# NSA attention of a hybrid decoder on one core: the compressed branch's values as two split products with a block-diagonal moving operand in place of four native fp32 products

## The chip, the core and the metric

The kernel runs on one core of one Trainium2 chip. Its engines work in parallel and each runs its own instructions in order: PE (TensorE, matrix products, with weight loads shown apart as PEld), DVE (VectorE), ACT (ScalarE), POOL (GpSimd), and SP, which issues transfers. Products accumulate in PSUM banks; PE, DVE and ACT can reach them. The metric is the device time of one launch in microseconds; the median of three runs was 2314.84.

## The reference

A decoder trunk of four layers on 512 tokens of width 1024: RG-LRU, native sparse attention (NSA), gated linear attention, RG-LRU, each followed by a SwiGLU channel mixer. The change touches NSA alone, layer 1. Cut to what matters there:

```python
kc = nsa_compress(k_c, ...)            # 31 compressed keys per kv group
vc = nsa_compress(v_c, ...)            # 31 compressed values per kv group, 64 wide
# for each block of 128 queries, 4 kv groups g, 4 heads h in a group:
lg_c = einsum('bqghd,bngd->bghqn', qi, kc) + head_bias(dist_c)
p_c = masked_softmax(lg_c, dist_c >= 0)
o_c = einsum('bghqn,bngd->bqghd', p_c, vc)      # the product that is changed
# o_s: selected blocks (all 8 blocks are chosen), o_w: sliding window, both over 512 keys
return gi[..., 0:1] * o_c + gi[..., 1:2] * o_s + gi[..., 2:3] * o_w
```

Each softmax weight is already multiplied by its gate before the products, so the three branches add up in one PSUM bank.

## The kernel before

Everything is computed transposed: features on partitions, 512 tokens in the free dimension. Weights stream in as blocks of 128x1024 (`wr`, `wc`), are split into a high and a low part of type fp32r by ACT and DVE (`ws`, L287 and L288), and a product of fp32 quality is three fp32r products (L329 to L331, L591 to L593). Where an operand is used unsplit, PE runs its native fp32 product.

The NSA attention loop (`attention`, `run`, L1159) goes over 32 units (g, i, br): 4 groups g of heads, 4 query blocks i, and two branches, br = 0 (selected together with compressed) and br = 1 (window). In a group the order is (3,0), (0,0), (3,1), (0,1), (2,0), (1,0), (2,1), (1,1) for (i,br). In iteration n three units are in work:

- `logits(n + 3)`: PE multiplies queries and keys (L1029, L1030; for br = 0 the 31 compressed keys lie in front of the 512 others, tile `kk`), DVE adds the bias and takes the row minimum of the negated logits (L1032, L1186), ACT takes exponentials (L1046, L1052);
- `weights(n + 2)`: DVE makes reciprocals and gate factors (L1001, L1002, L1065, L1066, L1068), POOL scales the weights L (L1060);
- `values(n)`: PE transposes the weights of 128 keys and four heads into one bank (L1116), ACT and DVE copy or split it (`ph`, `pl`: L357, L358), and up to four steps later PE multiplies the values with it into the bank `ob` (L1103, or L1105 and L1106). `store` then adds the two halves of `ob` and splits the result (L1136, L1137, L1143, L1144).

For br = 0, `values` first transposes the compressed weights of four heads (tile `lc`, four heads by 32 on the free axis) in one product (L1095), so that partition 32*hh + n holds key n of head hh, and ACT copies that to `pc` (L1097). The values of the compressed branch are `vcd`, a large tile of 128x4x4x64: for head hh, rows 32*hh to 32*hh + 31 hold the values and all other rows are zero. Four native fp32 products per unit (L1108, L1109), each with 128 moving columns, go into columns of rows 0 to 63 of `ob`.

PE's instructions of the loop stand in the order in which they are written (a manual schedule, L951). On ACT, DVE, POOL and SP a scheduler orders the instructions by its own estimate of when each is ready, and takes the tiles of a pool as they come free. The pool of large tiles has four buffers; `ktl`, `kth` (compressed keys' inputs), `vcd`, `kk` and `wc` (weight blocks that are summed during loading, of the feed-forward layers) share them. `no` and `nq` are output and query projections that fill PE inside the loop.

Of the kernel before, what the change touches and what calls it, by code (L numbers as in the profile page):

```python
# [8 lines left out]
F32 = mybir.dt.float32  # L9
F32R = mybir.dt.float32r  # L10
I32 = mybir.dt.int32
AF = mybir.ActivationFunctionType
OP = mybir.AluOpType
# [179 lines left out]
class Kernel:  # L193
# [615 lines left out]
    def nsa(self, j, nxt):  # L809
        nc, prm = self.nc, self.prm  # L810
        mm = nc.tensor.matmul
# [3 lines left out]
        nsm = self.fixed.tile([128, 256], F32, name="nsm")  # L815
# [22 lines left out]
        def hidden(kv, lo, hi):  # L838
            w1 = self.take(("raw", "w1", j, kv))
            b = self.bank("cmp")  # L840
            o = b[0:64, 0:124].rearrange("p (g n) -> p g n", n=31)
            for m in range(16):
                mm(o, lhsT=w1[:, m * 64:m * 64 + 64],
                   rhs=lo[:, m, :, 0:31] if m < 8 else hi[:, m - 8, :, 1:32], start=m == 0, stop=m == 15)
            g = gl[kv] = self.slot("gl")
            nc.gpsimd.memset(g[:, 0:128], 0.0)
            glv = g[0:64, 0:128].rearrange("p (g n) -> p g n", n=32)
            nc.scalar.activation(glv[:, :, 0:31], o, AF.Gelu_apprx_tanh, bias=prm[0:64, C_B1 + kv:C_B1 + kv + 1])
# [7 lines left out]
        def cmp_spread():  # L856
            g4 = gl[2] = self.slot("gl4")
            nc.gpsimd.tensor_copy(g4[0:64].rearrange("p (g h n) -> p g h n", g=4, h=4),
                                  gl[1][0:64, 0:128].rearrange("p (g n) -> p g n", n=32)[:, :, None, :].to_broadcast([64, 4, 4, 32]))
            nc.gpsimd.memset(vcd, 0.0)  # L860

        def cmp_values():
            b = self.bank("cmp2")
            for g in range(4):
                mm(b[:, g * 64:g * 64 + 64], lhsT=gl[2][0:64, g * 128:g * 128 + 128], rhs=nsm[0:64, 128:192], start=True, stop=True)
            for hh in range(4):
                rows = slice(hh * 32, hh * 32 + 32)
                nc.vector.tensor_tensor(vcd[rows, :, hh, :], b[rows, 0:256].rearrange("p (g d) -> p g d", d=64),
                                        nsm[rows, None, 192:256].to_broadcast([32, 4, 64]), op=OP.add)

        def gates(b):
            gf = self.slot("gf")
# [39 lines left out]
        b = self.bank("ng")  # L912
# [6 lines left out]
        at(1, cmp_keys)  # L919
        list(queries(1))  # L920
        hidden(1, *c1)
        vcd = self.large([128, 4, 4, 64], "vcd")
        cmp_spread()
        at(1, cmp_values)
        for i in range(4):
            at(i + 1, bias_rows, 4 * i)
# [14 lines left out]
        for t in range(4):  # L941
            r = self.rstd[:, t:t + 1]
            for br in range(2):
                v = V[t, br] = self.slot("v", F32R)
                vv = v.rearrange("p (g two d) -> p g two d", g=4, two=2)
# [10 lines left out]
    def attention(self, j, kc, kw, qw, V, vcd, gt, os, queries, output):  # L956
        nc, mm = self.nc, self.nc.tensor.matmul
# [37 lines left out]
        LC = [self.fixed.tile([128, 128], F32, name=f"lc{i}") for i in range(4)]  # L995
        for x in LC:
            nc.gpsimd.memset(x, 0.0)

        def weight(g, i, br, s):
            r, w = small("sr"), small("sw")  # L1000
            nc.vector.reciprocal(r, s)  # L1001
            nc.vector.tensor_tensor(w, r, gt[:, i, g * 12 + br:g * 12 + 12:3], op=OP.mult)  # L1002
            return w
# [82 lines left out]
        def values(u, es):  # L1086
            g, i, br = u
            d = st.pop(u)
# [3 lines left out]
            ob = OB[g, i]  # L1092
            if br == 0:
                b = self.bank("pc")
                nc.tensor.transpose(b[:, 0:128], d["lc"][:, 0:128], self.ident)  # L1095
                pc = self.slot("pc")
                nc.scalar.activation(pc[:, 0:128], b[:, 0:128], AF.Copy)  # L1097

            def product(jt, p):
                v = V[jt, br][:, g * 128:g * 128 + 128]  # L1100
                first, last = br == 0 and jt == 0, br == 1 and jt == i
                if len(p) == 1:
                    mm(ob, lhsT=v.bitcast(F32), rhs=p[0], start=first, stop=last)  # L1103
                else:
                    mm(ob, lhsT=v, rhs=p[0], start=first, stop=False)  # L1105
                    mm(ob, lhsT=v, rhs=p[1], start=False, stop=last)  # L1106
                if br == 0 and jt == 0:
                    for hh in range(4):  # L1108
                        mm(ob[0:64, hh * 128:hh * 128 + 128], lhsT=vcd[:, g, hh, :], rhs=pc[:, 0:128], start=False, stop=False)  # L1109

            ne = len(es)
            for jt in range(i + 1):
                b = self.bank("pt")
                for hh in range(4):
                    c = slice(hh * 128, hh * 128 + 128)
                    nc.tensor.transpose(b[:, c], L[hh][:, jt * 128:jt * 128 + 128], self.ident)  # L1116
                if NSA_AT["whole"][g] >> (jt + 4 * br) & 1:
                    p = [self.slot("p")]
# [4 lines left out]
                else:  # L1123
                    p = self.split(b, "p")
# [346 lines left out]
```

## Time and profile before

| | |
|---|---|
| median of 3 runs | 2314.84 us (2314.52 to 2316.72) |
| profiled execution, its own time | 2313.41 us |
| its span | 2311.7 us |
| PE busy | 2275.7 us (98%) |
| DVE busy | 1483.2 us (64%) |
| ACT busy | 1221.9 us (53%) |
| POOL busy | 346.9 us (15%) |
| the attention loop | about 655 to 860 us of the span |

Busy shares of the whole span mix phases with different limits: outside the attention loop PE is fed without a break, inside it three more engines are nearly full. So the loop is read by itself, from the busy time in its stretches, from the chain of waits that ended last (each piece is followed back to what released it), and from single instructions in order of time. Records of PE overlap, since products are pipelined and their ends are modelled; what one of them costs PE is the distance from its start to the next start.

### The profile page before, as it was taken

The page shows a single profiled execution, that of the slowest core. Times are in us where ns is not written, and L with a number is a line of the kernel's source. Part 1 is how long each engine was busy: PE and PEld are TensorE (multiplying, and loading weights), DVE is VectorE, ACT ScalarE, POOL GpSimd, SP SyncE. Part 2 cuts the span into 40 slices and gives each one's busy share as a digit, 9 for nine tenths or more (in the row PEclk, how much of TensorE's full clock was granted, in tenths as well). Part 3 has the DMA queues.
Part 4 walks back from the last instruction along what each step waited for, and adds up shares of the span by engine and source line. Part 5 has one row for each costly group of instructions (what it writes and reads, how often), then busy time and mean ns, then how long its engine had stood idle before and what let it go on. Part 6 is the DMA issues. An engine that isn't in the chain of part 4 may idle for free.

```text
span 2311.7 us, 29407 instructions
## 1 busy us (share of the span) xinstructions
PE 2275.7 (98%) x10898; PEld 1912.0 (83%) x10898; DVE 1483.2 (64%) x2460; ACT 1221.9 (53%) x1971; POOL 346.9 (15%) x413
## 2 busy tenths in 40 slices
PE   8999999999999999999999999999999999999998
PEld 7877888898876778888988887888898878888897
DVE  7887646466289888555466526745465886745555
ACT  5965535353468766444455435625354685635353
POOL 1001101001356531010110000101010000201010
PEclk9999999999999999999999999999999999999999
DMA  9246858452431137666573223958485324957561
GB/s 287 86 119 172 205 135 196 108 151 88 171 83 28 47 86 198 172 149 175 133 217 98 82 74 111 217 137 190 129 201 165 98 67 138 216 146 178 143 142 66
DMA packets 99455, 323.84 MB, mean 140 GB/s; under 512 B 11248, under 2 KB 18032, under 8 KB 99312
## 3 DMA queue, kind: packets, MB, share of 16 engines
q1 hardware_dynamic: 70512, 225.49, 29.0%
q0 software_dynamic: 28800, 96.48, 24.0%
q8 instruction: 85, 1.39, 0.2%
q14 instruction: 58, 0.48, 0.1%
HBM read 316.68 MB, written 5.24 MB: 139 GB/s over the span
## 4 chain that ended last, share of the span: by engine, by line
PE 86%; DVE 8%; ACT 4%; issue 1%; POOL 0%; DMA 0%; SPq 0%; POOLq 0%; DVEq 0%; ACTq 0%
PE pj L331 9%; PE pj L330 9%; PE pj L329 9%; PE b L592 8%; PE b L593 8%; PE b L591 8%; PE t L592 3%; PE t L593 3%; PE t L591 3%; PE lp L329 2%; PE lp L331 2%; PE lp L330 2%; PE at L663 2%; DVE ws L288 1%; DVE L L1032 1%
## 5 line engine op out<-in xcount | busy, mean ns | idle before, releaser
L288 DVE TENSOR_TENSOR ws<-wr,ws 128x1024 fp32r<-128x1024 f32 (+1 forms) x402 | 474.9, 1184 | 416.9 <-ACT ws L287 414.1
L287 ACT ACTIVATE ws<-wr 128x1024 fp32r<-128x1024 f32 (+1 forms) x402 | 409.7, 1021 | 496.4 <-PE pj L331 206.5
L330 PE MATMUL pj<-al,ws 128*128 128x512 f32 (+1 forms) x728 | 278.7, 383 | 0.0
L329 PE MATMUL pj<-ah,ws 128*128 128x512 f32 (+1 forms) x728 | 278.7, 384 | 0.0
L331 PE MATMUL pj<-ah,ws 128*128 128x512 f32 (+1 forms) x728 | 278.4, 382 | 0.0
L288 DVE TENSOR_TENSOR ws<-wc,ws 128x1024 fp32r<-128x1024 f32 (+1 forms) x144 | 163.2, 1133 | 134.7 <-ACT ws L287 133.4
L287 ACT ACTIVATE ws<-wc 128x1024 fp32r<-128x1024 f32 (+1 forms) x144 | 142.2, 987 | 129.2 <-PE pj L331 70.9
L330 PEld LDWEIGHTS pj<-al,ws 128*128 128x128 f32 x728 | 136.9, 188 | 27.0 <-DVE al L358 1.1
L331 PEld LDWEIGHTS pj<-ah,ws 128*128 128x128 f32 x728 | 136.8, 188 | 26.5
L329 PEld LDWEIGHTS pj<-ah,ws 128*128 128x128 f32 x728 | 136.9, 188 | 26.1
L293 POOL DMA_DIRECT2D wc<-wall x88 | 80.2, 913 | 439.7 <-DVE ws L288 431.5
L250 POOL DMA_DIRECT2D wc<-wall x64 | 57.6, 900 | 575.0 <-DMA wc<-wall 273.6
L591 PE MATMUL b<-ws,ph 128*128 128x512 f32 (+1 forms) x384 | 143.4, 373 | 0.0
L592 PE MATMUL b<-ws,xh 128*128 128x512 f32 (+1 forms) x384 | 142.7, 372 | 0.0
L593 PE MATMUL b<-ws,xl 128*128 128x512 f32 (+1 forms) x384 | 142.5, 371 | 0.0
L592 PE MATMUL b<-ws,ph 128*128 128x512 f32 (+1 forms) x384 | 142.4, 371 | 0.0
L593 PE MATMUL b<-ws,pl 128*128 128x512 f32 (+1 forms) x384 | 142.4, 371 | 0.0
L591 PE MATMUL b<-ws,xh 128*128 128x512 f32 (+1 forms) x384 | 142.4, 371 | 0.0
L329 PE MATMUL lp<-xh,ws 128*128 128x512 f32 x320 | 125.8, 393 | 6.6 <-ACT ws L287 6.6
L331 PE MATMUL lp<-xh,ws 128*128 128x512 f32 x320 | 124.6, 392 | 3.4 <-DVE ws L288 3.4
L330 PE MATMUL lp<-xl,ws 128*128 128x512 f32 x320 | 125.3, 391 | 0.0
L541 DVE TENSOR_TENSOR h<-h,pj 128x512 f32<-128x512 f32 x116 | 77.4, 683 | 36.3 <-PE pj L331 36.3
(374 smaller groups left out, 5231.3 us busy)
## 6 DMA issues: line engine op xcount, KB each, us to landing
wr<-wall SPq DMA_DIRECT2D x322, 512.0 KB, 4.1
wc<-wall POOLq DMA_DIRECT2D x104, 512.0 KB, 7.0
wc<-wall SPq DMA_DIRECT2D x40, 512.0 KB, 4.0
wc<-wall POOLq DMA_DIRECT2D x48, 384.0 KB, 6.2
wr<-wall SPq DMA_DIRECT2D x48, 384.0 KB, 3.1
wr<-wall POOLq DMA_DIRECT2D x32, 512.0 KB, 6.1
wc<-wall SPq DMA_DIRECT2D x16, 384.0 KB, 3.0
wr<-wall POOLq DMA_DIRECT2D x16, 384.0 KB, 6.2
```

The lines of the kernel that those rows point to most:

```text
L250: self.nc.gpsimd.dma_start(self.raw[i][:, 0:n], self.wall[b][:, 0:n], accum_op=OP.add)
L287: self.nc.scalar.activation(hi, r, AF.Copy)
L288: self.nc.vector.tensor_tensor(lo, r, hi.bitcast(F32), op=OP.subtract)
L293: self.nc.gpsimd.dma_start(whole[:, 0:n], self.wall[self.uses[on][2][0]][:, 0:n], accum_op=OP.add)
L329: mm(ps, lhsT=wh, rhs=x[0], start=first, stop=False)
L330: mm(ps, lhsT=wh, rhs=x[1], start=False, stop=False)
L331: mm(ps, lhsT=wl, rhs=x[0], start=False, stop=last)
L541: nc.vector.tensor_tensor(self.h[m + c], self.h[m + c], banks[c], op=OP.add)
L591: mm(o, lhsT=xh, rhs=wh, start=first and k == 0, stop=False, skip_group_check=True)
L592: mm(o, lhsT=xh, rhs=wl, start=False, stop=False, skip_group_check=True)
L593: mm(o, lhsT=xl, rhs=wh, start=False, stop=k == 3, skip_group_check=True)
L663: nc.tensor.transpose(b[:, i * 128:i * 128 + 128], rows[i][:, c * 128:c * 128 + 128], self.ident)
```

## The change

`vcd` becomes an ordinary slot of type fp32r, 4 groups by a high and a low part by 64 columns, with the same values on all four blocks of 32 rows (no zeros). One stationary operand of 128 columns is then high and low part side by side, and its product lands in both halves of `ob`, which `store` adds. The zeros go over to the moving operand: `PD`, two large tiles of 128x2x512 that alternate by query block, zeroed once by POOL. In each unit with br = 0 ACT copies each head's block of 32 rows and 128 columns into its place on the diagonal (high part `ph`), and POOL writes the difference pc - ph into the second tile (`pl`). Two products of 512 columns replace the four native ones.

```diff
-            nc.gpsimd.memset(vcd, 0.0)
 def cmp_values():
-            for hh in range(4):
-                rows = slice(hh * 32, hh * 32 + 32)
-                nc.vector.tensor_tensor(vcd[rows, :, hh, :], b[rows, 0:256].rearrange("p (g d) -> p g d", d=64),
-                                        nsm[rows, None, 192:256].to_broadcast([32, 4, 64]), op=OP.add)
+            t = self.slot("vcf")
+            tv = t[:, 0:256].rearrange("p (g d) -> p g d", d=64)
+            nc.vector.tensor_tensor(tv, b[:, 0:256].rearrange("p (g d) -> p g d", d=64),
+                                    nsm[:, None, 192:256].to_broadcast([128, 4, 64]), op=OP.add)
+            nc.scalar.activation(vcd[:, :, 0], tv, AF.Copy)
+            nc.vector.tensor_tensor(vcd[:, :, 1], tv, vcd[:, :, 0].bitcast(F32), op=OP.subtract)
...
-        vcd = self.large([128, 4, 4, 64], "vcd")
+        vcd = self.slot("vcd", F32R).rearrange("p (g two d) -> p g two d", g=4, two=2)
...
+        PD = [self.large([128, 2, 512], "pd", F32R) for _ in range(2)]
+        for x in PD:
+            nc.gpsimd.memset(x.bitcast(F32), 0.0)
...
                 nc.scalar.activation(pc[:, 0:128], b[:, 0:128], AF.Copy)
+                ph, pl = PD[i % 2][:, 0], PD[i % 2][:, 1]
+                for hh in range(4):
+                    r, c = slice(hh * 32, hh * 32 + 32), slice(hh * 128, hh * 128 + 128)
+                    nc.scalar.activation(ph[r, c], b[r, 0:128], AF.Copy)
+                    nc.gpsimd.tensor_tensor(pl[r, c], pc[r, 0:128], ph[r, c].bitcast(F32), op=OP.subtract)
...
                 if br == 0 and jt == 0:
-                    for hh in range(4):
-                        mm(ob[0:64, hh * 128:hh * 128 + 128], lhsT=vcd[:, g, hh, :], rhs=pc[:, 0:128], start=False, stop=False)
+                    vv = vcd[:, g].rearrange("p two d -> p (two d)")
+                    mm(ob, lhsT=vv, rhs=ph, start=False, stop=False)
+                    mm(ob, lhsT=vv, rhs=pl, start=False, stop=False)
```

Where the rows stand on the engines. On ACT, at the first unit of group 1 (block 3, br = 0): `pc` is the copy of the transposed compressed weights, `L` the exponentials, `ph` the high parts of transposed weights, `o` the first halves of a stored result. Before:

```order
L1046 ACTIVATE L_5912,ssum_5930<-L_5912,m_5909 128x512
L1046 ACTIVATE L_5913,ssum_5930<-L_5913,m_5909 128x512
L1097 ACTIVATE pc_6000<-pc_5998 128x128
L1046 ACTIVATE L_5971,ssum_5988<-L_5971,m_5970 128x128 x3
L357 ACTIVATE ph_6017<-pt_6012 128x512
L1046 ACTIVATE L_5971,ssum_5988<-L_5971,m_5970 128x128
L1136 ACTIVATE o_6023<-ob_5683 64x256
L357 ACTIVATE ph_6038<-pt_6033 128x512
L1136 ACTIVATE o_6023<-ob_5683 64x256
L357 ACTIVATE ph_6049<-pt_6044 128x512
L1136 ACTIVATE o_6055<-ob_5781 64x256
```

and now:

```order
L1050 ACTIVATE L_5939,ssum_5957<-L_5939,m_5936 128x512
L1050 ACTIVATE L_5940,ssum_5957<-L_5940,m_5936 128x512
L1101 ACTIVATE pc_6027<-pc_6025 128x128
L1105 ACTIVATE pd_4905<-pc_6025 32x128 x4
L1050 ACTIVATE L_5998,ssum_6015<-L_5998,m_5997 128x128
L357 ACTIVATE ph_6052<-pt_6047 128x512
L1050 ACTIVATE L_5998,ssum_6015<-L_5998,m_5997 128x128
L1146 ACTIVATE o_6058<-ob_5698 64x256
L357 ACTIVATE ph_6073<-pt_6068 128x512
L1050 ACTIVATE L_5998,ssum_6015<-L_5998,m_5997 128x128
L1146 ACTIVATE o_6058<-ob_5698 64x256
L357 ACTIVATE ph_6084<-pt_6079 128x512
```

The four copies `pd` stand right behind `pc`, ahead of the exponentials of the next unit and the first `ph` of this one.

On POOL, in group 0 at the unit (2,0): `qq` are the low parts of the next group's four query tiles, `L` the scaled weights, `kk` the low parts of keys for a later group. Before:

```order
L986 TENSOR_TENSOR qq_5501<-qw_4617,qq_5501 64x512
L986 TENSOR_TENSOR qq_5504<-qw_4617,qq_5504 64x512
L1060 TENSOR_TENSOR L_5441<-L_5441,sw_5535 128x384
L1060 TENSOR_TENSOR L_5442<-L_5442,sw_5535 128x384
L1060 TENSOR_TENSOR L_5443<-L_5443,sw_5535 128x384
L1060 TENSOR_TENSOR L_5444<-L_5444,sw_5535 128x384
L986 TENSOR_TENSOR qq_5599<-qw_4649,qq_5599 64x512
L986 TENSOR_TENSOR qq_5602<-qw_4649,qq_5602 64x512
L975 TENSOR_TENSOR kk_6544<-kw_4891,kk_6544 64x512
L976 TENSOR_TENSOR kk_6544<-kw_4891,kk_6544 64x512
L1060 TENSOR_TENSOR L_5508<-L_5508,sw_5628 128x256 x2
L1060 TENSOR_TENSOR L_5509<-L_5509,sw_5628 128x256 x2
```

and now:

```order
L1064 TENSOR_TENSOR L_5452<-L_5452,sw_5552 128x384
L987 TENSOR_TENSOR qq_5518<-qw_4617,qq_5518 64x512
L1064 TENSOR_TENSOR L_5453<-L_5453,sw_5552 128x384
L987 TENSOR_TENSOR qq_5521<-qw_4617,qq_5521 64x512
L1064 TENSOR_TENSOR L_5454<-L_5454,sw_5552 128x384
L1064 TENSOR_TENSOR L_5455<-L_5455,sw_5552 128x384
L976 TENSOR_TENSOR kk_5929<-kw_4890,kk_5929 64x512
L977 TENSOR_TENSOR kk_5929<-kw_4890,kk_5929 64x512
L1064 TENSOR_TENSOR L_5525<-L_5525,sw_5643 128x256
L987 TENSOR_TENSOR qq_5614<-qw_4649,qq_5614 64x512
L1064 TENSOR_TENSOR L_5525<-L_5525,sw_5643 128x256
L987 TENSOR_TENSOR qq_5617<-qw_4649,qq_5617 64x512
```

The four `qq` are now spread out between the weights, and the last one stands behind both `kk` and a half of the next unit's weights; in before these `kk` belong to group 3, now to group 2, and those of group 3 come in group 1, where there were none.

On POOL again, at the end of the loop (weights of the last units, then the added loads `wc` for the feed-forward layer). Before:

```order
L1060 TENSOR_TENSOR L_7538<-L_7538,sw_7678 128x256 x2
L1060 TENSOR_TENSOR L_7539<-L_7539,sw_7678 128x256 x2
L1060 TENSOR_TENSOR L_7653<-L_7653,sw_7740 128x384
L1060 TENSOR_TENSOR L_7654<-L_7654,sw_7740 128x384
L1060 TENSOR_TENSOR L_7655<-L_7655,sw_7740 128x384
L1060 TENSOR_TENSOR L_7656<-L_7656,sw_7740 128x384
L1060 TENSOR_TENSOR L_7717<-L_7717,sw_7807 128x256 x2
L1060 TENSOR_TENSOR L_7718<-L_7718,sw_7807 128x256 x2
L250 DMA wc_8004<-wall 128x1024 x2
```

and now:

```order
L1064 TENSOR_TENSOR L_7627<-L_7627,sw_7765 128x256 x2
L1064 TENSOR_TENSOR L_7628<-L_7628,sw_7765 128x256 x2
L1106 TENSOR_TENSOR pd_4904<-pc_7837,pd_4904 32x128 x4
L1064 TENSOR_TENSOR L_7740<-L_7740,sw_7827 128x384
L1064 TENSOR_TENSOR L_7741<-L_7741,sw_7827 128x384
L1064 TENSOR_TENSOR L_7742<-L_7742,sw_7827 128x384
L1064 TENSOR_TENSOR L_7743<-L_7743,sw_7827 128x384
L1064 TENSOR_TENSOR L_7804<-L_7804,sw_7902 128x256 x2
L1064 TENSOR_TENSOR L_7805<-L_7805,sw_7902 128x256 x2
L1106 TENSOR_TENSOR pd_4905<-pc_7912,pd_4905 32x128 x4
L250 DMA wc_8044<-wall 128x1024 x2
```

A run of four differences `pd` stands ahead of the last two units' weights, and another behind them, ahead of the added loads.

## Rows read from the trace of the kernel before

**Rows 1.** Busy us by engine in the loop's four groups; PEclk, DMA share, GB/s.

```profile
655.00:705.00 50.00, 48.29 (x260) 35.81 (x258) 47.78 (x193) 39.15 (x121) 34.85 (x43) 1.00 0.24 62
705.00:750.00 45.00, 42.47 (x239) 31.36 (x238) 42.27 (x179) 37.18 (x115) 32.51 (x42) 1.00 0.16 36
750.00:806.00 56.00, 52.80 (x297) 41.50 (x296) 50.26 (x191) 43.96 (x126) 32.51 (x41) 1.00 0.19 48
806.00:860.00 54.00, 51.63 (x289) 41.77 (x288) 47.00 (x146) 36.69 (x104) 22.57 (x32) 1.00 0.33 75
```

After the window and its length the columns are PE, PEld, DVE, ACT and POOL.

**Rows 2.** Chain of waits, 655 to 860 us: by line, and the pieces of L1109.

```profile
by line: DVE L L1032 12.1%; DVE pl L358 12.0%; ACT L L1046 10.4%; DVE sw L1002 6.1%; issue 5.6%; DVE ol L1144 4.2%; DVE o L1137 3.5%; ACT ph L357 3.4%; DVE ws L288 3.4%; PE pt L1116 2.9%; DVE h L904 2.4%; DVE sc L1066 2.4%; DVE lc L1068 2.1
...
725.74 1.02 PE ob L1109 x8
...
817.62 1.02 PE ob L1109 x8
...
845.51 1.02 PE ob L1109 x8
```

**Rows 3.** PE in order of time: start, us, engine, line, output and inputs.

```profile
704.07 1.09 PE L1109 MATMUL ob<-pc,vcd 128*64 128x128 f32 x8
...
705.42 0.39 PE L1030 MATMUL qk<-kl,qq 128*128 128x512 f32 x1
705.65 0.39 PE L1029 MATMUL qk<-kh,qq 128*128 128x512 f32 x1
```

**Rows 4.** ACT and DVE in order of time; in brackets idle time and releaser.

```profile
698.56 0.25 ACT L1097 ACTIVATE pc<-pc 128x128 f32<-128x128 f32 x1
698.72 0.71 ACT L1046 ACTIVATE L<-L,m 128x512 f32<-128x512 f32 x1
...
743.88 0.69 DVE L358 TENSOR_TENSOR pl<-pt,ph 128x512 fp32r<-128x512 f32 x1 [0.21 <-ACT ph L357]
```

**Rows 5.** POOL by line, the loop; one line of the whole run (min/median/max ns).

```profile
L986 POOL TENSOR_TENSOR qq<-qw,qq 64x512 fp32r<-64x512 f32 x12 | 15.4, 1284 | 0.9
...
L978 POOL TENSOR_TENSOR kk<-kc,kk x4: 245/577/1116, 583.6 to 698.1; 128x32 fp32r<-128x32 f32 x4
```

**Rows 6.** DVE by line, L1002's spread, one stall and POOL beside it.

```profile
L1002 DVE TENSOR_TENSOR sw<-sr,gt 128x4 f32<-128x4 f32 x48 | 18.2, 385 | 1.0
L1066 DVE TENSOR_SCALAR sc<-sc 128x4 f32<-128x4 f32 x16 | 7.2, 452 | 0.1
...
L1002 DVE TENSOR_TENSOR sw<-sr,gt x48: 145/166/2985, 658.4 to 838.8; 128x4 f32<-128x4 f32 x48
...
825.84 2.98 DVE L1002 TENSOR_TENSOR sw<-sr,gt 128x4 f32<-128x4 f32 x1
825.33 3.46 POOL L1060 TENSOR_TENSOR L<-L,sw 128x384 f32<-128x384 f32 x4
```

**Rows 7.** POOL, PE and DVE in order of time around group 0.

```profile
668.74 6.45 POOL L1060 TENSOR_TENSOR L<-L,sw 128x512 f32<-128x512 f32 x8 [4.41 <-ACT L L1046]
673.74 1.09 PE L1109 MATMUL ob<-pc,vcd 128*64 128x128 f32 x8
684.87 2.62 POOL L986 TENSOR_TENSOR qq<-qw,qq 64x512 fp32r<-64x512 f32 x2
691.76 0.47 PE L1029 MATMUL qk<-kk,qq 128*128 128x512 f32 x1
696.42 0.68 DVE L1032 CUSTOM_DVE_ANT_0 L<-qk,bias 128x512 f32<-128x512 f32 x1
```

**Rows 8.** POOL and PE in order of time, last units.

```profile
837.53 6.56 POOL L1060 TENSOR_TENSOR L<-L,sw 128x384 f32<-128x384 f32 x8 [1.72 <-ACT L L1046]
845.44 1.09 PE L1109 MATMUL ob<-pc,vcd 128*64 128x128 f32 x8
```

**Rows 9.** The last added load of the loop, and the split that uses it.

```profile
856.40 0.86 POOL L250 DMA_DIRECT2D wc<-wall  x1 [4.93 <-DMA wc<-wall]
886.86 1.06 ACT L287 ACTIVATE ws<-wc 128x1024 fp32r<-128x1024 f32 x1 [0.30 <-PE b L593]
```

## Prediction

> **What bounds the kernel now.** I read the stretches first, then the chain of waits, then single rows. The change touches one stage, the attention loop, about 655 to 860 us of a 2311.7 us span. Cut into its four groups of heads [rows 1], the clock is full, PE reads as busy 94 to 97%, but those ends are modelled and overlap; DVE is busy 96, 94, 90 and 87%, ACT 68 to 83%, POOL 42 to 72%. Which of these sets the time is told by the chain [rows 2]: its biggest lines are DVE's and ACT's (logits L1032, low parts L358, exponentials L1046, the small L1002), the first PE line has 2.9%. Adding its 712 pieces up by engine gives about 115 of 205 us to DVE (56%), 45 to ACT (22%), 31 to PE (15%), 10 to POOL (5%). Of the sixteen groups of L1109, the products that the change replaces, three stand in it. So this stage waits for DVE and ACT; PE waits for them.
>
> **What is removed and added, per unit with br = 0 (there are 16).**
>
> PE. Four native products, eight records, take 1.02 us from their start to the next start [rows 2, 3]. A split product of 512 columns follows another at 0.23 us (705.42 to 705.65 [rows 3]); two make 0.46. That is 0.56 us less, 9 us over 16 units. It counts only where PE is late: three groups of L1109 are on the chain, 3 x 0.56 = 1.7 us. Ends: 0 and 9 us. Taken: **-1.7**.
>
> ACT. Four copies of 32x128 out of PSUM into the block-diagonal tile, right behind the copy pc. The trace has no copy on 32 partitions; the nearest is pc itself, 128x128 from the same bank: 0.25 us long, but the next instruction starts 0.16 after it (698.56 to 698.72 [rows 4]). Time goes with columns, so I take 0.16: 4 x 0.16 x 16 = 10.2 us of ACT (16 us at 0.25). What is queued behind them are the exponentials and the high part ph of the transposed weights, for which DVE's pl waits: at 743.88 it had been idle 0.21 us for ACT's ph [rows 4], one unit behind a pc. ACT's own idle time covers the rest, since it waits for DVE's maxima later in each unit. By ACT's share of the chain: 10.2 x 0.22 = **+2.2**; ends 0 (always covered) and 10.
>
> POOL. Four differences pc - ph of 32x128, ready only when those copies are. Two full operands on 512 columns cost 1284 ns, on 32 columns 245 ns at best [rows 5]; on the line between them 128 columns cost about 0.45 us. Four: 1.8 us, all: 29 us, against 122 us of POOL work in the four stretches [rows 1]. It reaches the end in two ways.
>
> First through DVE. A 128x4 product of operands in SBUF, L1002, has a median of 166 ns and a longest of 2985 ns [rows 6]. That longest one starts at 825.84 and ends at 828.82, where the POOL run of four differences of 825.33 ends, at 828.79: DVE stood until POOL was through. With 0.16 as the free price, L1002's 48 cost 10.2 us too much and L1066's 16 cost 4.6: 15 us lost over 122 us of POOL, 0.12 per us. For 29 us more: 3.5 us of DVE, by its share of the chain x 0.56 = **+2.0**; ends 0 and, if each of 16 runs of 1.8 us catches DVE for half its length, 14. The Trainium skill, page "SBUF — State Buffer", section "SBUF: two separate sides", names the cause: GpSimd and a DVE instruction with two SBUF inputs share a port pair that is an exclusive lock, held for one whole instruction. By that, a new difference could hold DVE for 0.45 us at most; the row of 2.98 us outlasts three POOL instructions of 0.86, so the trace shows longer stalls than the rule, and I keep the measured rate.
>
> Then through order. PE's second new product needs the last difference, and PE is in order, so transposes and logits of later units stand behind it. Mostly there is room: in the unit of [rows 3, 4] pc starts at 698.56 and L1109 at 704.07. Three places are short. (a) First unit: POOL's four slices of 512 from 668.74 end at 672.8, the differences at 674.6; PE's second product would go at 673.74 + 0.23 [rows 7]: 0.6 late. (b) End of group 0: POOL is busy without a break. Before, the fourth query tile qq of the next group was done at 684.87 + 2.62 = 687.5; now it stands behind two runs of differences (3.6), both kk (2.6) and two half slices (1.2), as the order shows: 694.9 at the latest, and PE took it at 691.76 [rows 7]. Of these 3 us DVE hides most, since it comes to these logits only at 696.42 [rows 7]: I take 0.9. (c) Last units: the run from 837.53 to 844.1 [rows 8] gets one run of differences ahead of it (part of it in 1.72 us of idle) and one behind: done between 846.0 and 847.8; PE wants it at 845.44 + 0.23. 0.3 to 2.1 late, 1.2 taken; this L1109 is on the chain, with nothing behind to hide it. Together **+2.7**; ends 0 and 6.
>
> Moved at no cost: the zeroing on POOL (two tiles instead of one) and the split of vcd lie before the loop, under PE's projections. Two of four large buffers are now held by the zeroed tiles, so the kk of groups 2 and 3 are made later (2.6 us of POOL more inside group 1, where POOL is idle for 12 of 45 us [rows 1]), and the loads of the wc tiles on SP and their added loads on POOL come later. The last added load of before was issued at 856.40 and its split began at 886.86 [rows 9], so 30 us of output and feed-forward work cover that; without that cover each late load would be waited for in full.
>
> Sum: -1.7 + 2.2 + 2.0 + 2.7 = **+5.2 us**. The profiled run took 2313.41 us (span 2311.7 and 1.7 around it), so 2318.6 for it; the median of the runs is 1.43 above that run. Against the median: 2314.84 + 5.2 = **2320.0 us**.
>
> **Rivals.**
> A, faster: PE is the bound after all. For it: its busy share, and the last two groups hold the projections that fill PE (`no`), with two of the three L1109 on the chain. Then the saving counts in full and the added work sits in idle time of ACT (48 us over the stage) and POOL (83 us): up to -9, about 2306 to 2310. Against it: 15% of the chain. It decides once L1109 is on the chain in more than half the units.
> B, nothing to be measured: additions are covered, PE's gain is not on the path; -4.6 to +4.6, 2310 to 2319. For it: no added instruction is DVE's, which bounds the stage. The terms that I took at a half or a fifth fall to 0, or PE's gain doubles.
> C, much slower: each run of differences holds DVE, as at 825.84. Sixteen times 0.9 us is 14, with the late products 2 to 6 more, less 2 to 4 for PE: +10 to +18, 2325 to 2333. It decides from about half of the runs on. Against it: most L1002 are not held (median 166 ns). The page's rule of one whole instruction would cap this at 16 x 0.45 = 7 us, 2322.
> The change cannot fail to do what it says: PE's rows show both prices side by side, with the same kind of operands.
>
> **How the numbers follow.** A measurement of this kernel tells about 0.2%, 4.6 us, from no change. My sum lies just above that, so its neighbours share much of the chance: forecast (+4.7 to +10) 0.38, B 0.36, A 0.17, C 0.09. Slower by over 0.2%: 0.38 + 0.09 = 0.47; the same 0.36; faster 0.17. The range for 8 in 10 leaves out the better half of A and the worse half of C: 2309 to 2328. The forecast's own range is 2319.5 to 2325.
>
> **What would show it.** PE: a group of the two new products should take 0.46 to 0.6 us from start to next start. ACT: copies pd at some 0.16 us each back to back, ACT's busy time in the stage up by 10 to 16. POOL: differences near 0.45 us, busy time up by 25 to 33. DVE: busy time up by 2 to 5 although it gets no instruction, in L1002, L1066 and L1144. Waits: PE before the second new product for POOL's pd, in the first and last units. The stage should end 4 to 8 us later, the stages behind it unchanged in length. I am wrong if the loop ends earlier (A: PE had been late in more places than the chain shows), if PE waits for pd in most units (C), or if the feed-forward stage is longer (the wc loads).

## The result: slower, 2332.1 us

| | before | after |
|---|---|---|
| median (runs) | 2314.68 us (4) | 2332.07 us (4) |
| ratio, 95% interval | | 1.0074, 1.0062 to 1.0086 |
| span of the profiled run | 2311.7 us | 2330.6 us |
| PE, DVE busy | 2275.7, 1483.2 us | 2275.5, 1483.7 us |
| ACT, POOL busy | 1221.9, 346.9 us | 1238.4, 376.0 us |

The kernel takes 17.4 us longer. The direction was the forecast's, the size was not: +5.2 was forecast, and 2332.1 lies above the range of 2309 to 2328.

The loss lies in the attention loop alone. Its last products of the compressed branch started at 845.44 us before [rows 8]; after, they start at 863.86. The stages behind the loop are as long as they were. The busy time in the loop's stretches, in the columns of [rows 1] (the last stretch reaches to the loop's later end):

```profile
655.00:705.00 50.00, 42.33 (x205) 30.81 (x203) 41.53 (x159) 35.83 (x110) 39.74 (x54) 0.97 0.23 60
705.00:750.00 45.00, 38.27 (x188) 27.26 (x186) 37.81 (x152) 39.11 (x122) 34.25 (x48) 0.96 0.05 13
655.00:877.30 222.30, 193.22 (x973) 145.80 (x972) 185.76 (x700) 172.89 (x526) 154.05 (x222) 0.98 0.20 50
```

Before, DVE was busy 47.78 of the first 50 us [rows 1]; now 41.53. The engine that led the chain of the stage stands idle: 36.5 us over the loop (222.30 - 185.76), 17.7 before (205.00 - 187.32). What it waits for is in the table of waits (engine, line, what it waited for: us in all, times, longest), 655 to 880 us:

```profile
ACT L L1050 <- DVE m L1036: 21.4, 15, 3.6
DVE pl L358 <- ACT ph L357: 18.1, 26, 4.0
...
POOL pd L1106 <- ACT pd L1105: 9.3, 8, 2.4
...
DVE o L1147 <- ACT o L1146: 4.7, 11, 0.7
ACT pc L1101 <- POOL qq L987: 4.7, 2, 2.4
...
PE qk L1033 <- ACT pd L1105: 3.1, 4, 1.2
...
PE ob L1119 <- POOL pd L1106: 0.7, 1, 0.7
```

The second row was 3.9 us before, the first was longer, 27.9 us. The chain of waits, 655 to 880 us, has changed hands against [rows 2]: ACT's exponentials lead it, the high part `ph` and the new copies `pd` are in it, DVE's logits are down from 12.1% to 3.7%. Added up by engine, each piece once, ACT has gone from 42 us to 89, DVE from 112 to 52, POOL from 9 to 26.

```profile
by line: ACT L L1050 16.0%; ACT ph L357 7.6%; issue 6.7%; DVE pl L358 6.0%; ACT pd L1105 5.1%; POOL L L1064 4.9%; POOL qq L987 4.0%; DVE L L1036 3.7%; DVE ol L1154 3.2%; PE no L329 2.9%; PE pt L1126 2.8%; ACT o L1146 2.6%; PE no L330 2.5%; 
```

The added instructions themselves, one unit in order of time (start, duration, engine, line):

```profile
677.41 0.26 ACT L1101 ACTIVATE pc<-pc 128x128 f32<-128x128 f32 x1
677.56 1.13 ACT L1105 ACTIVATE pd<-pc 32x128 fp32r<-32x128 f32 x4
678.71 0.62 ACT L1050 ACTIVATE L<-L,m 128x384 f32<-128x384 f32 x1
...
680.36 2.03 POOL L1106 TENSOR_TENSOR pd<-pc,pd 32x128 fp32r<-32x128 f32 x4
```

All of them by line (count, busy us, mean ns, idle before and its releaser):

```profile
L1105 ACT ACTIVATE pd<-pc 32x128 fp32r<-32x128 f32 x64 | 16.9, 264 | 1.2
L1106 POOL TENSOR_TENSOR pd<-pc,pd 32x128 fp32r<-32x128 f32 x64 | 30.5, 477 | 13.1 <-ACT pd L1105 9.3
L1118 PE MATMUL ob<-pd,vcd 128*128 128x512 f32 x16 | 9.7, 608 | 0.0
L1119 PE MATMUL ob<-pd,vcd 128*128 128x512 f32 x16 | 6.6, 414 | 0.7 <-POOL pd L1106 0.7
```

A copy of 32 partitions is as long as one of 128 (0.26 us) and does not run into the next: from 677.56 the next instruction starts 1.15 us later, 0.29 a copy. That is 18.4 us of ACT in 16 units. Where ACT, POOL and PE wait for one another, around the end of group 0:

```profile
692.88 0.19 ACT L1050 ACTIVATION_READ_ACCUMULATOR L<-L,m 128x1 f32 x1
695.39 0.28 ACT L1101 ACTIVATE pc<-pc 128x128 f32<-128x128 f32 x1 [2.32 <-POOL qq L987]
695.56 1.13 ACT L1105 ACTIVATE pd<-pc 32x128 fp32r<-32x128 f32 x4
...
694.07 1.29 POOL L987 TENSOR_TENSOR qq<-qw,qq 64x512 fp32r<-64x512 f32 x1
...
696.84 0.48 PE L1033 MATMUL qk<-kk,qq 128*128 128x512 f32 x1 [1.16 <-ACT pd L1105]
```

ACT wants a free buffer for `pc`. By the releaser that the trace names, it gets one when POOL has finished its last query tile, whose source frees it, at 695.36; until then ACT stands 2.32 us, and everything behind it in its program with it. Then PE waits 1.16 us for the bank that the four copies read.

### The profile page after: what moved, and what is told of

It is laid out like the page before. It is cut to its first block, busy times and chain, and to the rows that moved or that the text cites. A ratio compares the mean times of both kernels' runs of the same rounds, so it can differ in the third digit from the quotient of the medians.

```text
span 2330.6 us, 29313 instructions
## 1 busy us (share of the span) xinstructions
PE 2275.5 (98%) x10802; PEld 1908.8 (82%) x10802; DVE 1483.7 (64%) x2458; ACT 1238.4 (53%) x2036; POOL 376.0 (16%) x478
## 3 DMA queue, kind: packets, MB, share of 16 engines
q8 instruction: 85, 1.39, 0.2%
## 4 chain that ended last, share of the span: by engine, by line
PE 86%; ACT 6%; DVE 5%; issue 1%; POOL 1%; DMA 0%; POOLq 0%; DVEq 0%; SPq 0%; ACTq 0%
PE pj L331 9%; PE pj L330 9%; PE pj L329 9%; PE b L592 8%; PE b L591 8%; PE b L593 8%; PE t L592 3%; PE t L593 3%; PE t L591 3%; PE lp L329 2%; PE lp L331 2%; PE lp L330 2%; PE at L663 2%; ACT L L1050 2%; DVE ws L288 1%
```

## Experiments

The start of each unit's transposition of the compressed weights (`pc` on PE) is a clock for the loop. Every figure is its start less that of the kernel before, in us, at the first unit of groups 1, 2 and 3 and at the last unit (single profiled runs, so 1 us either way means little):

| kernel | group 1 | group 2 | group 3 | last | median less before |
|---|---|---|---|---|---|
| changed kernel | 6.9 | 14.8 | 17.8 | 16.6 | +17.4 |
| products alone (e1) | 0.2 | 2.4 | 2.2 | 0.8 | -2.7 |
| copies, no differences (e2) | 4.5 | 11.6 | 14.0 | 12.8 | +13.9 |
| differences, no copies (e3) | 3.1 | 7.7 | 7.8 | 5.6 | +5.5 |
| before + 4 copies on ACT (e5) | 3.6 | 8.0 | 9.7 | 10.9 | +13.0 |
| before + 2 copies on ACT (e10) | 3.3 | 5.5 | 5.1 | 7.3 | +3.7 |
| before + 4 copies on DVE (e11) | 6.7 | 8.3 | 8.1 | 8.9 | +6.4 |
| before + 4 differences on POOL (e6) | 4.0 | 5.8 | 7.2 | 5.4 | +5.3 |

My theory after the result: ACT's copies cost most, as ACT is no longer covered; POOL's differences cost through its own late work. The rivals: what the change moved (keys prepared later, buffers), PE behind the low half, the bank that the copies hold, the place of the copies, and DVE held by POOL.

### Taking the preparation away

```diff
# e1: both lines removed; e2: the second; e3: the first
-                    nc.scalar.activation(ph[r, c], b[r, 0:128], AF.Copy)
-                    nc.gpsimd.tensor_tensor(pl[r, c], pc[r, 0:128], ph[r, c].bitcast(F32), op=OP.subtract)
# e4
-                    mm(ob, lhsT=vv, rhs=pl, start=False, stop=False)
+                    mm(ob, lhsT=vv, rhs=ph, start=False, stop=False)
```

> The changed kernel with both preparations left out: no ScalarE copies into the high half, no GpSimd differences into the low half, so the two products multiply zeros and the compressed branch adds nothing to the output. What remains of the change is the two 512-column products, the two zeroed tiles, the values split in two and the later key preparation. If the loss of 17.4 us comes from the preparation on ScalarE and GpSimd, this takes 2309 to 2315 us: no more than the kernel before, less up to 16 x 0.6 us of TensorE. If it comes from what the change moved (the keys of a group prepared later, the buffer of the values, the order), it stays at 2326 to 2332 us.

2312.10 us, ratio 0.9989 (0.9981 to 0.9998): the products, with all that moved, are worth 2.7 us. What moved costs little: the row of the table of waits in which ACT waits for POOL's query tile (0.6 us before) is here too, and the unit clock loses 2.4 us by group 2 and has most of it back by the last unit (0.8).

```profile
ACT pc L1101 <- POOL qq L987: 2.5, 1, 2.5
```

> The changed kernel with the four GpSimd differences of a unit left out: the low half stays zero and its product is multiplied all the same. If ScalarE's four copies (1.13 us from the first's start to the end of the fourth, right behind the copy of the transposed weights and ahead of the next high part on the in-order ScalarE queue) carry the loss, it stays at 2326 to 2331 us. If GpSimd carries it (2.0 us a unit, 30 us in all, which make its query and key preparation late in the first two groups), it falls to 2313 to 2319 us. If both share it, because ScalarE's queue waits for buffers that GpSimd frees late, 2320 to 2325 us. If a port shared by VectorE and GpSimd were the cause, as the third rival of the prediction had it, it falls to about 2315 us and VectorE's busy time in the loop falls with it.

2328.68 us, 1.0057 (1.0044 to 1.0071). Leaving the differences out gives back 3.4 us only. Against the products alone the copies cost 16.6 us, nearly one for one for 16.9 us of busy ACT. DVE's wait for `ph`, in the table of waits, is nearly as long as in the changed kernel:

```profile
DVE pl L358 <- ACT ph L357: 17.2, 27, 2.6
```

> The changed kernel with ScalarE's four copies of a unit left out: the high half stays zero, the low half is the whole transposed weight, written by the four GpSimd differences as before. If ScalarE carries the loss, 2312 to 2318 us. If GpSimd carries it, 2324 to 2331 us. If both share it, 2318 to 2324 us. The sum of what this and the run without differences give back against 17.4 us tells whether the two add up (equal), cover one another (less) or need one another (more).

2320.25 us, 1.0023 (1.0013 to 1.0034): the differences alone cost 8.1 us over the products alone, and DVE's wait for `ph`, in the same table, is back at the value of before. PE waits 3.2 us for the differences here, 0.7 in the changed kernel; that may be part of the 8.1.

```profile
DVE pl L358 <- ACT ph L357: 4.0, 10, 1.3
PE ob L1118 <- POOL pd L1105: 3.2, 2, 1.7
```

The two cost 16.6 and 8.1 us alone and 20.0 together: they cover one another by 4.7 us, and ACT's is the larger.

> The changed kernel with the second product reading the high half again, so that TensorE never waits for GpSimd's differences, which are still made; the output misses the low part and has the high one twice. The trace of after shows TensorE behind the differences in 1.3 us in all, so 2330 to 2332 us if the loss lies in the engines' load. If the in-order TensorE behind the low half were what costs, 2314 to 2322 us.

2331.83 us, 1.0072 (1.0059 to 1.0084), as the changed kernel. In the changed kernel PE's wait for the low half costs nothing that can be measured.

### The dose alone, in the kernel before

Nobody reads the small tile here, so no wait of a product and no buffer of the change is in it. The order of the other instructions is not held fixed: the scheduler makes a new one with each edit.

```diff
+        dh = self.fixed.tile([128, 128], F32R, name="dh")
...
                 nc.scalar.activation(pc[:, 0:128], b[:, 0:128], AF.Copy)
+                for hh in range(4):                     # e10: range(2)
+                    r = slice(hh * 32, hh * 32 + 32)
+                    nc.scalar.activation(dh[r], b[r, 0:128], AF.Copy)
# e11 instead: nc.vector.tensor_copy(dh[r], b[r, 0:128])
# e6 instead:  nc.gpsimd.tensor_tensor(dl[r], pc[r, 0:128], pc[r, 0:128], op=OP.subtract)
```

> The kernel before, with its four native products, values and buffers as they were, and four copies of 32 rows more behind each copy of the transposed weights, into a small tile that nobody reads: ScalarE's dose alone, 16 x 1.1 us. Products, zeroed tiles, and waits for the copies are not in it. If ScalarE's time in this stage costs nearly one for one, as the copies' 16.6 us in the changed kernel suggest (2328.7 without differences against 2312.1 with the products alone), it takes 2328 to 2332 us. If the copies cost only because the products, or the two tiles that they write, wait for them, 2315 to 2319 us; the prediction's price (0.16 us a copy at ScalarE's share of 22% of the chain) would give 2317.

2327.95 us, 1.0056 (1.0043 to 1.0068), +13.0. The copies alone, without anything else of the change, do most of it. Its copies by line:

```profile
L1101 ACT ACTIVATE dh<-pc 32x128 fp32r<-32x128 f32 x64 | 16.9, 264 | 1.1
```

The table of waits:

```profile
ACT L L1047 <- DVE m L1033: 23.8, 17, 3.9
DVE pl L358 <- ACT ph L357: 15.4, 24, 2.0
```

The busy time of the loop, in the columns of [rows 1]:

```profile
655.00:873.00 218.00, 199.25 (x1068) 150.48 (x1068) 184.40 (x703) 171.83 (x524) 122.85 (x156) 0.98 0.22 52
```

ACT is idle for 46.2 of 218.0 us (218.00 - 171.83); before it was idle for 48.0 of 205.0 (sum of [rows 1]). Its idle time has hardly shrunk: 1.8 of some 15 us more work found room in it. It still waits 23.8 us for DVE's maxima, 27.9 before:

```profile
ACT L L1046 <- DVE m L1032: 27.9, 21, 4.5
```

The clock of PE is full from 655 to 806 us of this run, where most is lost, so a lower clock is not the cause.

One thing besides ACT's time is in this figure: the new order. With the unread copies the four `qq` of group 0 stand apart on POOL, as in the changed kernel, although no difference was added. The last one ends at 693.68 us, before at 687.49 [rows 7], with two copies (e10, below) at 692.59. The rows of the run with four copies and of that with two:

```profile
692.39 1.29 POOL L986 TENSOR_TENSOR qq<-qw,qq 64x512 fp32r<-64x512 f32 x1
...
691.30 1.29 POOL L986 TENSOR_TENSOR qq<-qw,qq 64x512 fp32r<-64x512 f32 x1
```

Leaving the added instructions aside, e2 and e4 have the order of the changed kernel on ACT, DVE and POOL, e1 and e3 share another, and that of e6 is nearly that of before. So the 3.4 us of e2 and the 8.1 of e3 compare kernels of one order; the 16.6 and 13.0 us of the copies hold their time and the order that comes with them. The order is not likely to be the larger part, since e10 has nearly the same order on POOL at 3.7 us and e12 another order on DVE at 12.5, but no run adds the copies to the order of before.

> The kernel before with two unread copies a unit instead of four, half the ScalarE dose that took 13.0 us. If ScalarE's time costs the same at every amount, 6.5 us: 2321 to 2322.5 us. If the first half is cheap, at the 22% of the chain of waits that ScalarE had before (16 x 0.55 us x 0.22 = 2 us), and the bound then moves to ScalarE: 2316.5 to 2318.5.

2318.73 us, 1.0017 (1.0008 to 1.0026), +3.7. Half the dose costs less than half, though the intervals leave a straight line just possible. DVE's wait for `ph` goes with the loss: 3.9 us at no copies, 7.4 at two, 15.4 at four, so +3.5 and +11.5, where the loss is 3.7 and 13.0 (in e12, below, the two part). The row at two, from the table of waits:

```profile
DVE pl L358 <- ACT ph L357: 7.4, 18, 1.5
```

> The kernel before with the same four unread copies a unit made by VectorE instead of ScalarE. VectorE had 56% of the chain of waits of this stage, ScalarE 22%. If the chain's share were the price of an engine's time, VectorE's dose would cost two and a half times ScalarE's for the same microseconds. If every microsecond that delays the alternation of the two engines costs alike, the price of a microsecond is about ScalarE's 0.72 (13.0 us for 16 x 1.13 us): 8 to 14 us for 11 to 18 us of copies, 2323 to 2329 us.

2321.47 us, 1.0030 (1.0019 to 1.0041), +6.4 for about as much busy time, less than expected. Its copies by line, and from the table of waits what DVE waits for `ph`:

```profile
L1101 DVE CAST dh<-pc 32x128 fp32r<-32x128 f32 x64 | 18.1, 284 | 1.7 <-ACT pc L1098 0.7
```

```profile
DVE pl L358 <- ACT ph L357: 0.8, 4, 0.2
```

So DVE, with 56% of the chain, is the cheaper engine (0.35 us per us), and ACT, with 22%, the dearer (0.77). DVE's wait for ACT is down from 3.9 us to 0.8, so some of its new work found room there.

> The kernel before, with four GpSimd subtractions of 32 rows more behind each copy of the transposed weights, into a small tile that nobody reads: GpSimd's dose alone, 16 x 2.0 us. If GpSimd's time costs through its own in-order work (weights and query preparation late), 2320 to 2325 us, as the 8.1 us of the run without copies suggest. If it costs only through TensorE's wait for the low half, 2314 to 2316 us.

2320.26 us, 1.0023 (1.0014 to 1.0031), +5.3 for 26.9 us of POOL, 0.20 per us, at the lower edge of what was expected, with no PE behind the results.

### Place and bank

```diff
# e8
-                    nc.scalar.activation(ph[r, c], b[r, 0:128], AF.Copy)
+                    nc.scalar.activation(ph[r, c], pc[r, 0:128], AF.Copy)
# e9: copies (from pc) and differences behind the loop over jt; e12: the same for the unread copies in the kernel before
```

> The changed kernel with the four copies reading the copy of the transposed weights in SBUF instead of the PSUM bank, at the same place of ScalarE's program: the bank is free some 1.1 us sooner, ScalarE's load is the same. The trace of after shows TensorE waiting 3.1 us in four places for a bank that these copies hold. If the bank costs, 2326 to 2329 us; if only ScalarE's load and order do, 2331 to 2333.

2333.97 us, 1.0082 (1.0068 to 1.0096): no gain. The bank is not the cause of the loss; as a copy from SBUF takes 304 ns, not 264, a gain of some 2 us could be hidden (by line):

```profile
L1105 ACT ACTIVATE pd<-pc 32x128 fp32r<-32x128 f32 x64 | 19.4, 304 | 1.2
```

> The kernel before with the four unread copies written behind the unit's transposes, so that on ScalarE they mostly stand behind the next exponentials or high parts, and read from SBUF; nobody waits for them. Their load is that of the run with the copies right behind the transposed weights (2328.0 us). If the place costs, ahead of the high parts that VectorE waits for, 2315 to 2321 us; if the load costs wherever it stands, 2326 to 2331.

2327.52 us, 1.0054 (1.0041 to 1.0067), +12.5, as with the copies at the earlier place. The load costs wherever it stands; behind the transposes it makes the exponentials late instead (ACT's L1047 has 16.4% of the chain, 12.5% with the early copies), and DVE waits 8.0 us for `ph`, half of its wait with the early copies, at nearly the same loss:

```profile
DVE pl L358 <- ACT ph L357: 8.0, 20, 1.4
```

> The changed kernel with the copies and differences written behind the unit's transposes instead of right behind the copy of the transposed weights, the copies reading that copy instead of the bank: on ScalarE's queue they then stand behind exponentials and high parts in most units, and the bank is free 1.1 us sooner. The load is the same. If their position costs (each high part, and VectorE behind it, late by the 1.1 us of the copies; VectorE waited 18.1 us for high parts, before 3.9) or the bank that they hold, 2316 to 2324 us. If ScalarE's load costs wherever it stands, 2328 to 2333 us.

2341.35 us, 1.0113 (1.0098 to 1.0129): neither outcome, 9 us more than the changed kernel. Here the low half does come too late for the in-order PE, which the same edit with unread copies (e12) cannot show (table of waits):

```profile
PE ob L1115 <- POOL pd L1139: 10.0, 5, 4.5
```

### The change's own copies on DVE, and another form

```diff
# e13; e14 leaves the differences out as well
-                    nc.scalar.activation(ph[r, c], b[r, 0:128], AF.Copy)
+                    nc.vector.tensor_copy(ph[r, c], b[r, 0:128])
```

> The same with the GpSimd differences left out, so that the low half stays zero. By the same prices 2312.1 us (the products alone) and 6.4 to 8: 2318 to 2321 us, against 2328.7 with ScalarE's copies. If VectorE, with the larger share of the chain before, were the dearer engine in the changed kernel, 2329 us or more.

2321.95 us, 1.0031 (1.0019 to 1.0042): 6.7 us less than with ACT's copies (e2), as the unread copies said (13.0 - 6.4 = 6.6). So the difference between the two engines, found in the kernel before, holds in the changed one. The price itself does not: over the products alone the copies cost 9.9 us on DVE and 16.6 on ACT, about 3.5 us more than unread ones (6.4 and 13.0), and what the rest is was not separated.

> The changed kernel with its four copies a unit made by VectorE instead of ScalarE; the copies, the differences and the products are otherwise those of the change. If the change loses by ScalarE's load, the price found with unread copies (6.4 us on VectorE, 13.0 on ScalarE) should carry over: 6 to 8 us less than the changed kernel, 2323 to 2326 us. If it loses by the chain from transposed weights through copies and differences to the product, whichever engine makes the copies, it stays at 2330 to 2334.

2328.91 us, 1.0063 (1.0051 to 1.0076): 3.2 us less, not 6 to 8. With the differences in it only half carries over. PE's wait for the low half is up from 0.7 to 3.3 us; whether that eats the other half was not separated.

```profile
PE ob L1119 <- POOL pd L1106: 3.3, 2, 1.9
```

> A third form of the same sum. The split is made before the transposition: VectorE writes the scaled weights rounded (the high part, in place of the in-place multiply), GpSimd makes the unrounded product and the low part (two operations of 128 x 124 at most), four transposes of 64 columns put the high part of all heads in rows 0 to 31 and the low part in rows 32 to 63 of one 64 x 512 tile, one ScalarE copy takes it over, and one product of 512 columns with 64 rows of the split values adds it. ScalarE has 0.33 us more a unit than before (0.585 us of a 128 x 512 copy against 0.26), not 1.1; TensorE has one product and three short transposes more. At ScalarE's price of one for one that is 16 x 0.33 = 5.3 us over the 2312.1 us of the products alone, or some 2 us less, as there is one product instead of two: 2313 to 2318 us. If GpSimd's two operations cost like the differences (8 us), 2320 to 2325.

```diff
-                nc.vector.tensor_tensor(v, v, w[:, :, None].to_broadcast([128, 4, nv]), op=OP.mult)
+                nc.vector.tensor_tensor(hl[:, :, 0, 0:nv], v, ww, op=OP.mult)
+                nc.gpsimd.tensor_tensor(v, v, ww, op=OP.mult)
+                nc.gpsimd.tensor_tensor(hl[:, :, 1, 0:nv], v, hl[:, :, 0, 0:nv].bitcast(F32), op=OP.subtract)
...
+                for hh in range(4):
+                    nc.tensor.transpose(b[0:64, hh * 128:hh * 128 + 128], LH[:, i, hh * 64:hh * 64 + 64].bitcast(F32), self.ident)
+                nc.scalar.activation(pc[0:64], b[0:64], AF.Copy)
...
+                    mm(ob, lhsT=vcd[0:64, g].rearrange("p two d -> p (two d)"), rhs=pc[0:64], start=False, stop=False)
```

2318.41 us, 1.0014 (1.0006 to 1.0023), just above the first range: 13.7 us less than the changed kernel, still 3.5 more than before. ACT has one copy of 0.58 us a unit (L1105) instead of `pc` and four (by line):

```profile
L1105 ACT ACTIVATE pc<-pc 64x512 fp32r<-64x512 f32 x16 | 9.2, 578 | 1.6 <-PE pc L1103 1.6
```

The prices fit it roughly: 2312.1 for the products alone, 0.32 x 16 = 5.1 us of ACT at the small dose's price of 0.45 (3.7 us for 8.3 busy) are 2.3, and POOL's two operations, 12.3 us in all, at 0.20 are 2.5: 2316.9, 1.5 us short. As even the products with their preparation left out gain only 2.7 us, no form tried here beats the kernel before.

## Why the prediction was wrong

**The step that failed is ACT's term.** It was +2.2, with ends of 0 and 10; alone it measures 13.0 (unread, before) to 16.6 us (in the changed kernel). Two factors were too low.

- *Duration.* 0.16 us a copy came from a copy of 128 partitions that the next exponential overlaps [rows 4], and from "time goes with columns". The four copies take 0.29 us each from start to start: 18.4 us, not 10.2; busy time in the whole run rose by 16.5, just past the end of what I looked for. This factor is 1.8, or 1.7 by the copies' 16.9 us of busy time, to which the prices below refer.
- *Price.* I multiplied by ACT's share of the chain, 0.22. Measured: 0.45 per busy us for the first half of the dose, 0.77 for the whole, and DVE, priced at 0.56, costs 0.35. This factor is 3.5, the larger one. The share says where the longest path ran once; it is no price for more work on an engine, and here it even ranks the two engines the wrong way round. It was also read a little high: with each piece of the chain counted once, DVE has 112 us of 205, ACT 42, PE 30, POOL 9, and 12 are "issue"; the terms would have been +2.1 and +1.9.

The sentence behind the price, that "ACT's own idle time covers the rest, since it waits for DVE's maxima later in each unit", is what the trace refutes: ACT was idle for 48.0 us before and for 46.2 with the unread copies and 13.0 us lost. Why its idle time stays is a reading, not a test: ACT and DVE hand work to each other (`ph` to `pl`, maxima to exponentials), so a later `ph` makes DVE late, DVE's maxima come later, and most of ACT's wait for them stays (27.9 us before, 23.8). The `ph` is not the only way: behind the transposes (e12) the same copies cost as much with half of DVE's wait. The row at 743.88 [rows 4], DVE already idle for ACT's `ph`, was the sign, and I used it as an illustration only.

**POOL's terms** were +2.0 and +2.7. Their durations held: 0.45 us a difference (median 452 ns), 2.03 us a run. Together the differences cost 5.3 us alone in the kernel before, 8.1 over the products alone, 3.4 beside the copies: near the sum by luck, since neither way was the one that I had priced. DVE's busy time in the loop did not rise (187.3 to 185.8 us in all). Its small product, which had cost 18.2 us with a longest of 2985 ns [rows 6], went down; by line in the loop, and its spread over the whole run (shortest, median, longest ns):

```profile
L1006 DVE TENSOR_TENSOR sw<-sr,gt 128x4 f32<-128x4 f32 x48 | 15.1, 317 | 0.6
```

```profile
L1006 DVE TENSOR_TENSOR sw<-sr,gt x48: 142/236/884, 658.1 to 857.1; 128x4 f32<-128x4 f32 x48
```

What this line and L1070 (L1066 before) saved, 5.1 us, other lines lost: the gated weights `lc` of L1072 and the splits of L1154 took 2.2 and 1.1 us more, and shape by shape DVE's instructions of the loop took 0.5 us more in all. So 30.5 us of new POOL work moved DVE's stall but hardly added to it, and the measured rate that I carried over was no rate. The longest of 0.88 us is no longer than one of POOL's slices of 512 columns (mean 1.05 us), where my row was 2.98 us; no run here explains either. The Trainium skill, page "SBUF — State Buffer", section "SBUF: two separate sides", states that the lock is held for one whole instruction. The row of 0.88 us fits that, the row of 2.98 us does not.

**The three short places.** (a) First unit: PE waited 0.67 us for the first low half, 0.6 forecast. The size is luck: POOL's first run took 2.89 us, not 1.8 (one of its four took 1.33), and ended 0.65 us later than forecast, and PE came later by about as much.

```profile
672.36 2.89 POOL L1106 TENSOR_TENSOR pd<-pc,pd 32x128 fp32r<-32x128 f32 x4
675.31 0.49 PE L1119 MATMUL ob<-pd,vcd 128*128 128x512 f32 x1 [0.67 <-POOL pd L1106]
```

(b) End of group 0: the last query tile ended at 694.07 + 1.29 = 695.36, 694.9 forecast: right as to the time. I had put it all in POOL's term. Without the differences (e2) the tile still ends at 693.57, with the products alone at 688.47 (685.85 + 2.62), so 5.1 us of the delay come with ACT's copies and the order that the scheduler makes of them, 1.8 with the differences. The rows of e2 and of e1:

```profile
692.28 1.29 POOL L987 TENSOR_TENSOR qq<-qw,qq 64x512 fp32r<-64x512 f32 x1
...
685.85 2.62 POOL L987 TENSOR_TENSOR qq<-qw,qq 64x512 fp32r<-64x512 f32 x2
```

That DVE would hide most was wrong, because the tile's end holds up ACT as well: it frees a buffer for `pc`, and ACT stood 2.32 us (once more for 2.41 at 746.18). These waits are not the differences' doing either: e2 has both (1.97 and 2.42 us), the products alone have the second (2.52).

(c) Last units: PE did not wait for the low half, 1.2 forecast. e4 says that PE's waits for the low half do not count.

**PE.** -1.7 forecast; the products alone gain 2.7 (0.5 to 4.4), with all that moved. Two products take 0.46 us from start to next start behind a split product, as forecast (groups 2 and 3). In groups 0 and 1 they take 0.86, but there the first of them starts earlier behind the native product ahead of it, so the stretch from that product to the instruction behind tells more: 1.98 us before (703.11 to 705.09), 1.32 now (710.47 to 711.79). The saving is 0.66 us, 0.56 forecast:

```profile
703.11 1.02 PE L1103 MATMUL ob<-p,v 128*128 128x512 f32 x2
705.09 0.50 PE L1029 MATMUL qk<-kh,qq 128*128 128x512 f32 x1
...
710.47 1.02 PE L1112 MATMUL ob<-p,v 128*128 128x512 f32 x2
710.93 0.79 PE L1118 MATMUL ob<-pd,vcd 128*128 128x512 f32 x1
711.56 0.39 PE L1119 MATMUL ob<-pd,vcd 128*128 128x512 f32 x1
711.79 0.40 PE L1033 MATMUL qk<-kh,qq 128*128 128x512 f32 x1
```

**Moved at no cost.** Right in the end: with the products alone the unit clock is up to 3.5 us late in group 2 but 0.8 at the last unit, and the run is not longer; in the changed kernel PE is busy 99.47 of the first 100 us behind the loop (877 to 977), as it was before (860 to 960).

**Rival C** gave the size (+10 to +18, though its own terms add up to +12 to +18) and the wrong mechanism: of DVE's instructions in the changed kernel that overlap a run of differences, only three are over 0.3 us longer than the shortest of their shape, by 0.7 at most. Rivals A and B fall. That PE waits for `pd` in most units, which I named as the sign of C, did not happen either; the sign that mattered, DVE behind `ph`, I had not listed.

What stays open: why ACT's second two copies cost 9.3 us for 8.6 busy and the first two 3.7 for 8.3. DVE's wait for `ph` shows where it goes, not why there is slack for one half and none for the other. With two and with four copies the order on ACT and DVE differs in some places, and what that is worth was not tested.

## What to carry to other kernels

An engine's share of the chain of waits is no price for more work on it: where two engines hand work back and forth, measure the price with unread copies of the same shape, which needs none of the real change, and look at the order that the scheduler makes with them. Another place for the copies did not help here (+12.5 us against +13.0). Idle time later in the cycle need not cover added work: here 1.8 of some 15 us found room in 48. To save 0.66 us of TensorE a unit at the price of four small ScalarE operations (1.15 us) was a bad trade in a stage where ScalarE feeds VectorE.

## What was not expected of the hardware

- ScalarE copies of 32x128 into disjoint rows of one tile take as long as one of 128x128 (264 and 261 ns) and follow one another at 0.29 us; the start to start of 0.15 us from `pc` to the first of them (677.41 to 677.56) is not kept among them. From SBUF they take 304 ns. One copy of 64x512 takes 578 ns, as 128x512 does (590).
- VectorE's copies of the same shape from PSUM take 284 ns.
- TensorE's granted clock was 1.00 throughout the loop before. In the changed kernel it was 0.83 in 695 to 705 us (0.50, its lower level, in 701 to 703), behind a stretch of 10 us in which the engine had been busy for 7.50 and 3 us in which it had been busy for 1.39; it was 0.83 again in 725 to 735, and 1.00 in between. With the unread copies on ACT it stayed at 1.00 to 806 us with over 8 us already lost, so there the loss needs no lower clock. What the low stretches add in the changed kernel was not separated.
